# Probabilities times values in float32, two heads of a pair side by side in the array

## The chip, the cores and the metric

One Trainium2 chip, one of its cores. The metric is device time in microseconds; lower is better. The kernel before took 3191.86 us, the median of three runs (3186.04 to 3200.37).

## What is computed

One inference step of a decoder with a convolution layer and an attention layer, for a prompt of 2048 tokens and eight sequences of four new tokens. The change concerns the prompt's attention alone: three groups of eight heads of 64, each group with its own window and dilation. Queries of 128 (a tile) see their own block of 128 keys and the one before:

```python
s = jnp.einsum('...nqd,...nkd->...nqk', qb, k_band, preferred_element_type=jnp.float32) * ATTN_SCALE
s = jnp.where(valid, s, NEG_INF)
mx = jnp.max(s, axis=-1, keepdims=True)
e = jnp.exp(s - mx)
den = jnp.sum(e, axis=-1, keepdims=True)
o = jnp.einsum('...nqk,...nkd->...nqd', e, v_band.astype(jnp.float32)) / den
lse = (mx + jnp.log(den))[..., 0]
```

All is float32. The group outputs are merged later by their `lse`. The last rows of keys and values are outputs too (the caches).

## The kernel before

The program runs in four stages: the convolution's input projections and the convolution (`phase_a`), its output projection (`phase_b`), projections and attention of the three head groups (`phase_c`), merge and output projection (`phase_d`). The framework plans the order of the instructions on each engine with a cost model of its own, before the run, and adds the waits; an engine keeps that order on the chip.

Large products are made in three float32r matmuls: each operand is split into a high half (rounded to float32r) and a low half (the rest), and high x high, high x low and low x high are summed in PSUM. ScalarE (ACT) makes the high half by a copy that rounds, VectorE (DVE) the low half by a subtraction.

`phase_c` calls `attend_group` for each of the three head groups. For each of 16 tiles, `front(i)` loads or transposes the rows of x, projects keys, values and queries (`Trunk.project`, L537 to L540, 24 matmuls each with 512 columns moving), normalises and rotates keys and queries, transposes them and splits them. The values go from PSUM straight into two buffers of three slots: high half by ACT (L769), low half by DVE (L770). For tiles whose rows are part of the cache output, 21 of 48, DVE adds the two halves again (L788) and SyncE (SP) writes the sum out (L789). Then `attention` of the tile before is issued, so that the planner can lay it beside the projections of the next one. Steps of the sample's attention (class `Sample`) are put between; its value products (L708) are plain float32 matmuls of 32 columns, one for each of four tokens, into four partition groups of one bank.

`attention(i, ...)` works on four pairs of heads; e is the head of a pair, and its 64 dimensions are rows 64e to 64e+63 of the transposed queries and keys. `halves` are the key blocks: one (nh = 1) for the first tile of a subsequence, two (nh = 2) for the others. Of the 48 tiles 21 have one block (1, 4 and 16 in the three groups) and 27 have two. Scores (L812) are matmuls of 64 rows, e = 0 and e = 1 in the two halves of the array. DVE adds the mask and finds the maximum (L818), ACT takes the exponential and its sum (L823). Then, part by part (one pair with two blocks, or two pairs with one), PE transposes the probabilities into the bank `pt` (L831), ACT copies them rounded (L834), DVE subtracts for the low half (L835), and three float32r matmuls for each pair and block (L840 to L842) multiply the values of both heads, 128 columns stationary, with the probabilities of both heads, 256 columns moving. Half of that result is needed: rows 0 to 63 for the first head, 64 to 127 for the second. ACT copies the one (L844) and DVE the other (L845) to `uts`. At the tile's end four transposes (L848) turn `uts` into `pu`, DVE copies it to `u` (L849), and `u` is written out.

PSUM banks in the stage: `pj` 3, `tr` 1, and in the first two head groups `s` 2, `pt` 1, `ut` 1 (`ut` and `pu` share the one); in the third `s` 1, `sm` 1 and two that `pt`, `ut` and `pu` share (L891 to L893).

Of the kernel before, what the change touches and what calls it, by code (L numbers as in the profile page):

```python
# [9 lines left out]
F32 = mybir.dt.float32  # L10
F32R = mybir.dt.float32r
AF = mybir.ActivationFunctionType
ALU = mybir.AluOpType
# [211 lines left out]
class Weights:  # L225
# [4 lines left out]
    def __init__(self, tc, d, pool, stage):  # L230
        self.d = d
        self.tc, self.nc, self.pool, self.stage, self.n, self.lo = tc, tc.nc, pool, stage, 0, 0
# [200 lines left out]
class Trunk:  # L433


    def __init__(self, tc, d, kc, pk, pf, pm, psum):
        self.tc, self.nc, self.d, self.pk, self.pool, self.front = tc, tc.nc, d, pk, pf, psum
        self.q, self.p = (pm.tile([128, 2, 2, 512], F32R, tag=t, name="qp_" + t) for t in ("mh0", "ml0"))
        self.turn = [0, 0]
        self.ident, self.mask, self.gk, self.gq = kc.ident, kc.mask, kc.knorm, kc.qnorm  # L440
        self.nkv, self.nb, self.rope_s, self.eps = kc.kvnorm, kc.bnorm, kc.rope_s, kc.eps
        self.ss = kc.ss
        self.rstd = pk.tile([128, 49], F32, name="rstd")
        self.scores = pk.tile([128, 3, 8, TS], F32, name="scores")
        self.sout = pk.tile([TS, 512], F32, name="sout")
# [285 lines left out]
def attend_group(tr, pool, gi, w, kt, vt, state):  # L731

    nc, d = tr.nc, tr.d
# [4 lines left out]
    kvo = d["kvp"][gi].rearrange("(q d) a c -> d q a c", d=dil)  # L738
# [1 line left out]
    nc.sync.dma_start(tab, d["rope"][gi])  # L740
    wk, wv, wq = w
    kth, ktl = kt
    vth, vtl = vt

    def reorder(i, x, nm):

# [9 lines left out]
    def front(i):  # L756
        r, b = divmod(i, nb)
        nm = f"{gi}_{i}"
        s = state["slot"] = (state["slot"] + 1) % 3
        x = tr.rows(gi, i, nm) if gi else tr.flip(i, 128, nm)  # L760
        xt = tr.halves(x)
        col = i + (17 + 16 * (gi - 1) if gi else 0)
        rstd = tr.rstd[:, col:col + 1]
        pk = tr.project(xt, wk, 128, "k" + nm)
        marks = [[tr.first]]
        kn = tr.headnorm(pk, rstd, tr.gk, tab[:, i], 128, "k", nm)
        marks[0] += tr.marks
        pv = tr.project(xt, wv, 128, "v" + nm)
        act = nc.scalar.activation(vth[:, s], pv, AF.Copy, scale=rstd)  # L769
        dve = nc.vector.scalar_tensor_tensor(vtl[:, s], pv, rstd, vth[:, s].bitcast(F32), op0=ALU.mult, op1=ALU.subtract)  # L770
        pq = tr.project(xt, wq, 128, "q" + nm)
        marks.append([tr.first, act, dve])
        qn = tr.headnorm(pq, rstd, tr.gq, tab[:, i], 128, "q", nm)
        if gi < 2:
            reorder(i, x, nm)
        tr.turn[0] ^= 1
        qh, ql = (tr.q[:, tr.turn[0], e].rearrange("p (a b) -> p a b", a=4) for e in range(2))
        for src, h, l, t in ((kn, kth[:, s], ktl[:, s], "k"), (qn, qh, ql, "q")):
            pt = tr.bank("tr", [128, 4, 128], f"p{t}t{nm}")
            for j in range(4):  # L780
                nc.tensor.transpose(pt[:, j], src[:, j * 128:j * 128 + 128], tr.ident)
            nc.scalar.copy(h, pt)
            nc.vector.tensor_tensor(l, pt, h.bitcast(F32), op=ALU.subtract)
        if r + dil * b * 128 >= first:
            o = slice(b * 128 - first // dil, b * 128 - first // dil + 128)
            nc.sync.dma_start(kvo[r, o, 0], kn)
            vo = tr.pool.tile([128, 512], F32, tag="sq", name=f"vo{nm}", bufs=1)
            nc.vector.tensor_tensor(vo, vth[:, s].bitcast(F32), vtl[:, s].bitcast(F32), op=ALU.add)  # L788
            nc.sync.dma_start(kvo[r, o, 1], vo)  # L789
        return (i, s, qh, ql), marks  # L790

    def attention(i, s, qh, ql):
        r, b = divmod(i, nb)
        nm = f"{gi}_{i}"
        p = (s + 2) % 3
        lo_s, hi_s = min(s, p), max(s, p)
        halves = [s] if b == 0 else [lo_s, hi_s]
        nh = len(halves)
# [3 lines left out]
        uts = pool.tile([128, 4, 128], F32, tag="uts", name=f"uts{nm}", bufs=1)  # L802

        rows = [slice(64 * e, 64 * e + 64) for e in range(2)]
        keys = [t[:, s:s + 1] if nh == 1 else t[:, lo_s:hi_s + 1:hi_s - lo_s] for t in (kth, ktl)]
        for js in [range(4)] if nh == 1 else [range(2), range(2, 4)]:

            sc = [tr.bank("s", [128, len(js), nh, 128], f"s{nm}_{js.start}{e}") for e in range(2)]
# [16 lines left out]
            for part in [js[:2], js[2:]] if nh == 1 else [js[:1], js[1:]]:  # L825
                w = len(part)
                pt = tr.bank("pt", [128, nh, w, 2, 128], f"pt{nm}_{part.start}")
                for k, j in enumerate(part):
                    for e in range(2):
                        for m in range(nh):  # L830
                            nc.tensor.transpose(pt[:, m, k, e], sms[e][:, j - js.start, m], tr.ident)  # L831
                tr.turn[1] ^= 1
                ph, pl = (tr.p[:, tr.turn[1], e].rearrange("p (m k e q) -> p m k e q", m=nh, k=w, e=2) for e in range(2))
                nc.scalar.copy(ph, pt)  # L834
                nc.vector.tensor_tensor(pl, pt, ph.bitcast(F32), op=ALU.subtract)  # L835
                ut = tr.bank("ut", [128, w, 2, 128], f"ut{nm}_{part.start}")
                for k, j in enumerate(part):
                    cs = slice(j * 128, j * 128 + 128)
                    for m, sl in enumerate(halves):
                        nc.tensor.matmul(ut[:, k], lhsT=vth[:, sl, cs], rhs=ph[:, m, k], start=(m == 0), stop=False)  # L840
                        nc.tensor.matmul(ut[:, k], lhsT=vth[:, sl, cs], rhs=pl[:, m, k], start=False, stop=False)
                        nc.tensor.matmul(ut[:, k], lhsT=vtl[:, sl, cs], rhs=ph[:, m, k], start=False, stop=(m == nh - 1))  # L842
                out = slice(part.start, part.stop)
                nc.scalar.copy(uts[rows[0], out], ut[rows[0], :, 0])  # L844
                nc.vector.tensor_copy(uts[rows[1], out], ut[rows[1], :, 1])  # L845
        pu = tr.bank("ut", [128, 4, 128], f"pu{nm}")
        for j in range(4):
            nc.tensor.transpose(pu[:, j], uts[:, j], tr.ident)  # L848
# [14 lines left out]
    for i in range(16):  # L863
        nxt, marks = front(i)
# [12 lines left out]
def phase_c(tc, d, tr, wts):  # L877
    nc = tc.nc
    with tc.tile_pool(name="c_p", bufs=2, reuse_waits="tile") as pool, \
            tc.tile_pool(name="c_t", bufs=1, reuse_waits="tile") as pt, ExitStack() as back:  # L880
        kt = [pt.tile([128, 3, 4, 128], F32R, name=f"kt{i}") for i in range(2)]
        vt = [pt.tile([128, 3, 512], F32R, name=f"vt{i}") for i in range(2)]

        def switch(**banks):

# [8 lines left out]
        for gi in range(3):  # L894
            w = [wts.block(d["wkv"][gi], f"k{gi}", tr.nkv), wts.block(d["wkv"][3 + gi], f"v{gi}", tr.nkv),
                 wts.block(d["wq"][gi], f"q{gi}", tr.nb)]
# [226 lines left out]
```

## Time and profile before

| | us |
|---|---|
| median of three runs | 3191.86 |
| the profiled execution's own time | 3187.62 |
| its span in the profile | 3185.8 |
| PE busy | 3054.5 (96%) |
| DVE busy | 2399.4 (75%) |
| ACT busy | 1533.8 (48%) |
| POOL busy | 1282.2 (40%) |

PE is TensorE, PEld its weight loads, POOL is GpSimd, SP the engine that issues most transfers. A busy time is the union of the records of an engine; PE's records overlap, since matmuls are pipelined and their ends are modelled, so what a matmul costs is seen in the distance between starts. A wait is idle time of an engine with what ended it.

### The profile page before, as it was taken

The page shows a single profiled execution, that of the slowest core. Times are in us where ns is not written, and L with a number is a line of the kernel's source. Part 1 is how long each engine was busy: PE and PEld are TensorE (multiplying, and loading weights), DVE is VectorE, ACT ScalarE, POOL GpSimd, SP SyncE. Part 2 cuts the span into 40 slices and gives each one's busy share as a digit, 9 for nine tenths or more (in the row PEclk, how much of TensorE's full clock was granted, in tenths as well). Part 3 has the DMA queues.
Part 4 walks back from the last instruction along what each step waited for, and adds up shares of the span by engine and source line. Part 5 has one row for each costly group of instructions (what it writes and reads, how often), then busy time and mean ns, then how long its engine had stood idle before and what let it go on. Part 6 is the DMA issues. An engine that isn't in the chain of part 4 may idle for free.

```text
span 3185.8 us, 43063 instructions
## 1 busy us (share of the span) xinstructions
PE 3054.5 (96%) x15694; PEld 2633.4 (83%) x15694; DVE 2399.4 (75%) x4067; ACT 1533.8 (48%) x3017; POOL 1282.2 (40%) x809
## 2 busy tenths in 40 slices
PE   6999999999999988999889999999999989999998
PEld 6999999999999976778668888778778777667786
DVE  6699999999989775766467777886678777556455
ACT  6545555554544273656434444644445534444432
POOL 1999988997888230000022222232222031001343
PEclk9999999999999998999989999999999999999999
DMA  6222333333232367566566666886566465552764
GB/s 178 85 85 92 99 120 116 108 104 98 92 145 64 115 216 164 159 174 178 124 183 169 173 175 168 233 218 170 139 147 172 133 186 175 182 174 97 246 235 168
DMA packets 563693, 482.39 MB, mean 151 GB/s; under 512 B 338609, under 2 KB 474417, under 8 KB 555929
## 3 DMA queue, kind: packets, MB, share of 16 engines
q1 hardware_dynamic: 560889, 475.64, 51.7%
q10 hardware_dynamic: 2592, 4.01, 0.3%
q8 instruction: 123, 2.02, 0.3%
q14 instruction: 89, 0.73, 0.1%
HBM read 345.42 MB, written 221.84 MB: 178 GB/s over the span
## 4 chain that ended last, share of the span: by engine, by line
PE 67%; DVE 13%; DMA 11%; ACT 4%; POOL 3%; issue 2%; SPq 1%; ACTq 0%; POOLq 0%; DVEq 0%
PE pg L68 4%; PE pg L70 4%; PE pg L69 4%; PE pv L68 3%; PE pv L70 3%; PE pv L69 3%; PE s L812 3%; PE pz L70 2%; PE pz L68 2%; PE pz L69 2%; DMA bc<-t_c 2%; PE pjq L539 2%; PE pjq L540 2%; PE pjq L537 2%; PE pjk L537 2%; PE pjv L539 2%
## 5 line engine op out<-in xcount | busy, mean ns | idle before, releaser
L181 POOL TENSOR_TENSOR ca<-ca,tp 128x1024 f32<-128x1024 f32 x288 | 705.8, 2453 | 159.2 <-ACT tp L180 108.3
L196 DVE SCALAR_TENSOR_TENSOR acc<-vb,cws,acc 128x1024 f32<-128x1024 f32 x608 | 754.2, 1281 | 6.4
L752 POOL COPY ro<-xt 128x512 f32<-128x512 f32 x128 | 147.6, 1160 | 838.2 <-ACT xt L501 456.9
L180 ACT ACTIVATE tp<-vb,cws 128x1024 f32<-128x1024 f32 x288 | 330.3, 1151 | 295.5 <-POOL ca L181 282.9
L630 POOL TENSOR_TENSOR qb<-qb,kc 128x512 f32<-128x512 f32 x96 | 129.8, 1355 | 335.5 <-DMA qb<-t_qs 252.2
L823 ACT ACTIVATE sm<-sm,ngm 128x256 f32<-128x256 f32 (+1 forms) x384 | 173.2, 453 | 153.8 <-DVE ngm L820 153.2
L68 PE MATMUL pg<-xh,wh 128*128 128x416 f32 x640 | 226.0, 353 | 3.4 <-ACT xh L151 3.4
L70 PE MATMUL pg<-xh,wl 128*128 128x416 f32 x640 | 226.7, 354 | 0.0
L68 PE MATMUL pv<-xh,wh 128*128 128x416 f32 x640 | 225.2, 352 | 1.1 <-DVE vb L109 0.8
L70 PE MATMUL pv<-xh,wl 128*128 128x416 f32 x640 | 226.0, 353 | 0.0
L70 PE MATMUL pz<-xh,wl 128*128 128x416 f32 x640 | 225.9, 353 | 0.0
L69 PE MATMUL pg<-xl,wh 128*128 128x416 f32 x640 | 224.9, 351 | 0.1
L68 PE MATMUL pz<-xh,wh 128*128 128x416 f32 x640 | 224.6, 351 | 0.0
L69 PE MATMUL pv<-xl,wh 128*128 128x416 f32 x640 | 223.6, 349 | 0.0
L69 PE MATMUL pz<-xl,wh 128*128 128x416 f32 x640 | 223.5, 349 | 0.0
L360 PE MATMUL bpo<-ho,bmh 128*128 128x512 f32 x512 | 206.0, 404 | 5.8 <-ACT ho L262 5.8
L361 PE MATMUL bpo<-lo,bmh 128*128 128x512 f32 x512 | 205.9, 403 | 2.6 <-POOL lo L265 2.1
L362 PE MATMUL bpo<-ho,bml 128*128 128x512 f32 x512 | 204.6, 401 | 0.7 <-DVE bml L337 0.7
L812 PE MATMUL s<-kt,qp_mh 64*128 64x256 f32 (+1 forms) x1152 | 164.0, 297 | 4.6 <-DVE u L818 4.1
L812 PEld LDWEIGHTS s<-kt,qp_mh 64*128 64x128 f32 x1152 | 129.7, 189 | 46.9 <-issue 26.1
L537 PE MATMUL pjk<-hk,xt 128*128 128x512 f32 x384 | 160.9, 419 | 0.4 <-DVE ptvs L533 0.4
L539 PE MATMUL pjv<-lv,xt 128*128 128x512 f32 x384 | 156.4, 407 | 0.0
(327 smaller groups left out, 7958.7 us busy)
## 6 DMA issues: line engine op xcount, KB each, us to landing
t_xt<-ro SPq DMA_DIRECT2D x128, 256.0 KB
xt<-t_xt SPq DMA_DIRECT2D x32, 1024.0 KB
wr<-in_win SPq DMA_DIRECT2D x48, 512.0 KB
qb<-t_qs SPq DMA_DIRECT2D x96, 256.0 KB
kc<-in_cache SPq DMA_DIRECT2D x72, 256.0 KB
vc<-in_cache SPq DMA_DIRECT2D x72, 256.0 KB
t_c<-ca SPq DMA_DIRECT2D x16, 1040.0 KB
bc<-t_c SPq DMA_DIRECT2D x16, 1024.0 KB
```

The costliest lines, as they stand in the source:

```text
L68: nc.tensor.matmul(ps, lhsT=hi[:, k], rhs=xh[:, k], start=(k == 0), stop=False)
L69: nc.tensor.matmul(ps, lhsT=hi[:, k], rhs=xl[:, k], start=False, stop=False)
L70: nc.tensor.matmul(ps, lhsT=lo[:, k], rhs=xh[:, k], start=False, stop=(k == 7))
L180: nc.scalar.activation(tp, src, AF.Copy, scale=cws[:, ct, j:j + 1])
L181: nc.gpsimd.tensor_tensor(dst, dst, tp, op=ALU.add)
L196: nc.vector.scalar_tensor_tensor(out if j == KT - 1 else acc[h], vt[:, h * 1024 + j:h * 1024 + j + 1024], cws[:, ct, j:j + 1], out if j == ...
L360: nc.tensor.matmul(po[:n], lhsT=mh[:, a], rhs=hi, start=(a == 0), stop=False)
L361: nc.tensor.matmul(po[:n], lhsT=mh[:, a], rhs=lo, start=False, stop=False)
L362: nc.tensor.matmul(po[:n], lhsT=ml[:, a], rhs=hi, start=False, stop=(a == 15))
L537: first = nc.tensor.matmul(ps[:n], lhsT=xh[:, j], rhs=hi[:, j], start=(k == 0), stop=False)
L539: nc.tensor.matmul(ps[:n], lhsT=xh[:, j], rhs=lo[:, j], start=False, stop=False)
L812: nc.tensor.matmul(sc[e][:, k], lhsT=q[rows[e], j], rhs=keys[t][rows[e], :, j], start=(n == 0), stop=(n == 2))
```

## The change

The values are kept once, in float32, and the probabilities too: the low halves are gone. The result bank `ut` is taken once for a tile, and for each pair and key block there are two float32 matmuls, one per head, with 64 stationary columns and 128 moving ones; they write rows 0 to 63 and 64 to 127 of the same columns of the bank. One ACT copy empties the bank at the tile's end. The cache's value rows are written from the value buffer itself. The buffer of the probabilities has four slots in place of two.

```diff
-        self.q, self.p = (pm.tile([128, 2, 2, 512], F32R, tag=t, name="qp_" + t) for t in ("mh0", "ml0"))
+        self.q = pm.tile([128, 2, 2, 512], F32R, tag="mh0", name="qp_q")
+        self.p = pm.tile([128, 4, 512], F32, tag="ml0", name="qp_p")
...
-        act = nc.scalar.activation(vth[:, s], pv, AF.Copy, scale=rstd)
-        dve = nc.vector.scalar_tensor_tensor(vtl[:, s], pv, rstd, vth[:, s].bitcast(F32), op0=ALU.mult, op1=ALU.subtract)
+        act = nc.scalar.activation(vt[:, s], pv, AF.Copy, scale=rstd)
         pq = tr.project(xt, wq, 128, "q" + nm)
-        marks.append([tr.first, act, dve])
+        marks.append([tr.first, act])
...
             nc.sync.dma_start(kvo[r, o, 0], kn)
-            vo = tr.pool.tile([128, 512], F32, tag="sq", name=f"vo{nm}", bufs=1)
-            nc.vector.tensor_tensor(vo, vth[:, s].bitcast(F32), vtl[:, s].bitcast(F32), op=ALU.add)
-            nc.sync.dma_start(kvo[r, o, 1], vo)
+            nc.sync.dma_start(kvo[r, o, 1], vt[:, s])
...
+        ut = tr.bank("ut", [128, 4, 128], f"ut{nm}")
         for js in [range(4)] if nh == 1 else [range(2), range(2, 4)]:
...
-                tr.turn[1] ^= 1
-                ph, pl = (tr.p[:, tr.turn[1], e].rearrange("p (m k e q) -> p m k e q", m=nh, k=w, e=2) for e in range(2))
-                nc.scalar.copy(ph, pt)
-                nc.vector.tensor_tensor(pl, pt, ph.bitcast(F32), op=ALU.subtract)
-                ut = tr.bank("ut", [128, w, 2, 128], f"ut{nm}_{part.start}")
+                tr.turn[1] = (tr.turn[1] + 1) % 4
+                x = tr.p[:, tr.turn[1]].rearrange("p (m k e q) -> p m k e q", m=nh, k=w, e=2)
+                nc.scalar.copy(x, pt)
+
                 for k, j in enumerate(part):
-                    cs = slice(j * 128, j * 128 + 128)
                     for m, sl in enumerate(halves):
-                        nc.tensor.matmul(ut[:, k], lhsT=vth[:, sl, cs], rhs=ph[:, m, k], start=(m == 0), stop=False)
-                        nc.tensor.matmul(ut[:, k], lhsT=vth[:, sl, cs], rhs=pl[:, m, k], start=False, stop=False)
-                        nc.tensor.matmul(ut[:, k], lhsT=vtl[:, sl, cs], rhs=ph[:, m, k], start=False, stop=(m == nh - 1))
-                out = slice(part.start, part.stop)
-                nc.scalar.copy(uts[rows[0], out], ut[rows[0], :, 0])
-                nc.vector.tensor_copy(uts[rows[1], out], ut[rows[1], :, 1])
+                        for e in range(2):
+                            c = j * 128 + 64 * e
+                            nc.tensor.matmul(ut[rows[e], j], lhsT=vt[:, sl, c:c + 64], rhs=x[:, m, k, e], start=(m == 0), stop=(m == nh - 1))
+        nc.scalar.copy(uts, ut)
         pu = tr.bank("ut", [128, 4, 128], f"pu{nm}")
...
-        vt = [pt.tile([128, 3, 512], F32R, name=f"vt{i}") for i in range(2)]
+        vt = pt.tile([128, 3, 512], F32, name="vt")
```

## Rows read from the trace of the kernel before

**Rows 1.** The page's part 4: the chain that ended last, shares of the span by engine

```profile
PE 67%; DVE 13%; DMA 11%; ACT 4%; POOL 3%; issue 2%; SPq 1%; ACTq 0%; POOLq 0%; DVEq 0%
```

**Rows 2.** Busy time of a stretch: start:end, length, PE, PEld, DVE, ACT, POOL, clock, DMA, GB/s

```profile
1600.00:2994.00 1394.00, 1349.46 (x7211) 1063.22 (x7211) 978.30 (x2766) 629.59 (x1763) 307.83 (x258) 0.98 0.62 171
```

**Rows 3.** Timeline of PE in one stretch: start, duration, engine, line, operation, tiles, count

```profile
1867.99 0.28 PE L840 MATMUL ut<-qp_ml,vt 128*128 128x256 f32 x1
1868.11 0.28 PE L841 MATMUL ut<-qp_ml,vt 128*128 128x256 f32 x1
...
1868.70 0.60 PE L831 MATMUL pt<-ident,sm 128*128 128x128 f32 x4
```

**Rows 4.** Timeline of PE's weight loads in the same stretch

```profile
1868.11 0.19 PEld L842 LDWEIGHTS ut<-qp_ml,vt 128*128 128x128 f32 x1
```

**Rows 5.** Groups by line and shape on PE: count, busy us, mean ns, idle before

```profile
L840 PE MATMUL ut<-qp_ml,vt 128*128 128x256 f32 x300 | 91.4, 305 | 9.5 <-DVE uts L845 6.1 <-ACT qp_ml L834 1.4 <-ACT yq L454 1.0
...
L708 PE MATMUL spo<-vc,spq 128*32 128x512 f32 x192 | 36.8, 602 | 0.0
```

**Rows 6.** Timeline of PE: one whole value product of the sample

```profile
2724.54 1.92 PE L708 MATMUL spo<-vc,spq 128*32 128x512 f32 x16
```

**Rows 7.** Timeline of PE: changes between full-array instructions and others, two places

```profile
1996.77 0.28 PE L842 MATMUL ut<-qp_ml,vt 128*128 128x256 f32 x1
1996.98 0.38 PE L812 MATMUL s<-kt,qp_mh 64*128 64x256 f32 x1
1997.29 0.66 PE L831 MATMUL pt<-ident,sm 128*128 128x128 f32 x4
...
2695.83 0.28 PE L840 MATMUL ut<-qp_ml,vt 128*128 128x256 f32 x1
2696.04 1.06 PE L708 MATMUL spo<-vc,spq 128*32 128x512 f32 x6
2697.03 0.39 PE L841 MATMUL ut<-qp_ml,vt 128*128 128x256 f32 x1
...
2700.17 1.90 PE L708 MATMUL spo<-vc,spq 128*32 128x512 f32 x10
```

**Rows 8.** Timeline of PE: first and last matmul of the 150 value groups

```profile
1643.36 0.38 PE L840 MATMUL ut<-qp_ml,vt 128*128 128x256 f32 x1
...
2991.77 0.28 PE L842 MATMUL ut<-qp_ml,vt 128*128 128x256 f32 x1
```

**Rows 9.** Groups by line and shape on DVE and ACT, 1600 to 3000 us

```profile
L835 DVE TENSOR_TENSOR qp_ml<-pt,qp_ml 128x512 fp32r<-128x512 f32 x150 | 103.2, 688 | 25.8 <-ACT qp_ml L834 24.0
L770 DVE SCALAR_TENSOR_TENSOR vt<-pjv,rstd,vt 128x512 fp32r<-128x512 f32 x47 | 35.1, 746 | 27.5 <-ACT vt L769 27.2
L845 DVE COPY uts<-ut 64x128 f32<-64x128 f32 x108 | 31.8, 295 | 23.7 <-ACT uts L844 20.8
L845 DVE COPY uts<-ut 64x256 f32<-64x256 f32 x42 | 18.0, 428 | 34.4 <-ACT uts L844 33.6
L788 DVE TENSOR_TENSOR vo<-vt,vt 128x512 f32<-128x512 f32 x21 | 15.0, 715 | 0.2
...
L834 ACT CAST qp_ml<-pt 128x512 fp32r<-128x512 f32 x150 | 87.4, 583 | 73.6 <-PE pt L831 72.2
```

**Rows 10.** What PE waited for, 1600 to 3000 us: total, times, longest

```profile
PE pqt L781 <- DVE hnq L565: 6.2, 6, 2.8
PE ut L840 <- DVE uts L845: 6.1, 6, 2.1
PE s L812 <- DVE u L818: 4.1, 4, 1.6
PE ut L841 <- DVE qp_ml L835: 3.8, 5, 1.5
PE pkt L781 <- DVE hnk L565: 3.8, 4, 1.7
PE pu L848 <- DVE uts L845: 2.3, 2, 1.6
```

More of the change, by code (lines that the diff above doesn't have):

```diff
@@ L742, in attend_group @@
     kth, ktl = kt
-    vth, vtl = vt
     def reorder(i, x, nm):
```

## The prediction, made before the changed kernel was run

> **What bounds the kernel now.** I read the views in this order: the chain that ended last, the busy time of the stretch that the change touches, the timeline of TensorE (PE) inside that stretch, then what PE waited for. The chain lies on PE for 67% of the span, with VectorE (DVE) far behind at 13% [rows 1]. All that the change touches runs between 1600 and 2994 us, where three groups of 16 tiles are projected and attended. There PE is busy for 1349.5 of 1394 us and DVE for 978.3, so PE sets the pace and DVE has slack on average [rows 2]. So an instruction taken from PE counts in full there, one taken from DVE only where PE waited for it. PE's busy time is modelled, though: what a matmul really holds is the distance between starts. Six float32r matmuls of one value group start at 1867.99 and the next transposes at 1868.70, so one holds PE for 0.118 us, although its record lasts 0.28 [rows 3]. The loads of their stationary operands hide: the load at 1868.11 starts with the matmul and runs 0.19 us beside it [rows 4].
>
> **Part 1, the product itself.** A tile has four head pairs and one or two key blocks; each "part" of the loop at L825 makes one group of six matmuls (L840 to L842, 128x256 moving). L840 counts 300, two to a group, so there are 150 groups [rows 5]. Today a group costs 6 x 0.118 = 0.71 us. Afterwards it has four calls: two column halves e, for two blocks m (or two pairs k), each with 128 columns moving in plain float32. The nearest rows for such a call are the sample's value products at L708: plain float32, 32 columns stationary, 512 moving, four calls to four column groups. The source makes 96 such calls and the trace has 192 records [rows 5]: each call is two passes. Sixteen of them stand as one piece of 1.92 us, one lasts 0.602, and they start in four waves, so a wave takes (1.92 - 0.602) / 3 = 0.44 us [rows 5, 6]. One behind another they would take 16 x 0.44 = 7.0 us. So passes to different column groups run side by side, and a wave with 512 columns takes 0.44 us, one with 128 a quarter, 0.11 us. The new group has eight passes on two column groups, hence four waves, 0.44 us. That saves 150 x (0.71 - 0.44) = 40 us. A wave could cost as much as today's 0.118: 5 us less saving.
>
> **Part 2, what reshaping the array costs.** The trace shows a price each time PE goes from instructions that fill the array to ones that use part of it, and back. A single score matmul (64 rows) between L842 at 1996.77 and transposes at 1997.29 takes 0.52 us where two normal steps would be 0.24, so 0.28 more, and the transposes behind it are drawn out too. The two waves of L708 between L840 at 2695.83 and L841 at 2697.03 take 1.20 us where 0.12 + 0.88 is work, so 0.20 more, and L841 itself lasts 0.39 instead of 0.28, because its load is laid bare: 0.31 in all [rows 7]. A round trip is thus 0.28 to 0.34 us, a side 0.14 to 0.17. Now the value groups fill the array and pay nothing beside projections and transposes; afterwards every group is a partial one. I went through the 150 groups from 1643.36 to 2991.77 [rows 8] in PE's order: 120 begin behind an instruction that fills the array and 115 end before one; the others touch score matmuls or sample work, where there is a change of shape already. So 235 sides are added. Behind most groups come float32 transposes, whose load is the cheaper one, and a load of 64 columns is half of 128, so I take 0.15: 235 x 0.15 = 35 us lost, with ends of 31 (0.13) and 40 (0.17). Parts 1 and 2 nearly cancel: 40 - 35 = 5 us gained on PE.
>
> **Part 3, what leaves DVE and ScalarE (ACT).** DVE loses the low half of the probabilities (L835, 103.2 us), the low half of the values (L770, 35.1), its half of the output copies (L845, 31.8 + 18.0) and the sum that rebuilt the values for the cache (L788, 15.0): 203 of 978 us [rows 2, 9]. ACT keeps L834 as a copy, loses 150 half copies at L844 and gets 48 copies of 128x512, some 0.58 us each like L834: 28 us [rows 9] on an engine that is busy for 629.6 of 1394 [rows 2]. I cost it at nothing; its cover is the projection matmuls that PE has beside it. If that cover is gone, PE's transposes `pu` wait for a whole copy in place of a half one, about 0.2 us in 48 tiles, 10 us at most.
> What the relief is worth is read from PE's waits. Two belong to what is taken away: `ut` for the copy out of the only bank, 6.1 us, and L841 for the low half, 3.8. Those 9.9 go: afterwards the bank is emptied once per tile, today two to four times. Four more are for DVE's other work: 6.2, 4.1, 3.8 and 2.3, together 16.4 [rows 10]. With a fifth less on DVE I give back a third of them, 5 us. Together 15 us; the ends are nothing (the planner may order the work so that other waits take their place) and 10 + 16 + about 5 for waits hidden under the modelled ends, 31.
>
> **Part 4, edits at nothing.** The value rows for the cache go out of the value tile itself, where today SyncE's issue queues behind DVE's sum; 21 tiles issue it, neither more nor larger transfers than now. It reads a buffer that is written again three tiles later, and a tile takes nearly 30 us (1394 over 48), so nobody waits for it. The square at L549 shares its buffer with that sum and is no longer held by its transfer; that only helps ACT. One `ut` bank is held from a tile's first value group to its copy. In the first two groups of heads it has a bank of its own, as now; in the third it shares two banks with `pt`, and the copy of `pt` to SBUF frees the other in time, with the projection of the next tile as cover. If that cover is gone, the score softmax of the next tile is late; it is in the 10 us above.
>
> **The sum.** -40 + 35 - 15 = -20 us. The profiled execution took 3187.6 us (span 3185.8); the median of the three runs is 3191.9, 4.2 above it. So 3187.6 - 20 + 4.2 = 3172 us, 0.6% below the median. Everything against it at once (waves of 0.118, sides of 0.17, no waits returned, 10 us for the copy): -35 + 40 + 10 = +15, 3207. Everything for it: -40 + 31 - 31 = -40, 3152. A difference under 0.5%, 16 us, can't be told from none here.
>
> **Rivals.**
> *The reshaping eats the gain and no wait comes back.* Only parts 1 and 2 count: -5 us, 3187. For it: PE idles little as it is, and a planned order has other work ready wherever a wait ended; against it: the 9.9 us of waits whose cause is removed.
> *The two halves don't run side by side: slower.* The place is the innermost loop over e. If the second pass of half 0 has to be through before half 1 begins, or the planner puts other work between the two, a group is eight steps of 0.11, 0.88 us against 0.71: +26 us; with the 35 of reshaping and 10 of waits returned +51, so 3243. It decides as soon as the group takes more than 0.71 - 35/150 + 15/150 = 0.58 us. Against it: the four waves of L708 [rows 6]; for it: those are four groups with long moving operands, and L708's own block was broken into six and ten, so that other work came between [rows 7].
> *The loads are laid bare in each wave.* If a pass had to wait for its own load, each of the 600 waves would grow by half of the 0.11 us that a bare load of 128 columns shows [rows 7], 0.055: 33 us, so -20 + 33 = +13, 3205, no visible difference. Against it: today's loads run beside a matmul on the same rows [rows 4]. The Trainium skill, page "TensorE: Matmul & The Clock Gate", section "Part 3: Packing small matmuls — row/col tiling", says that a load overlaps matmuls in flight only when it goes to another row group; by that rule this rival would hold, since both halves use all rows. The trace doesn't bear the rule out for full-array matmuls.
> *More of the waits come back.* PE has 44.5 us idle in the stretch [rows 2]; if most of it goes, -5 - 40 = -45, 3147. Against it: part of it is for transfers that the change leaves alone.
>
> **How the numbers follow.** Forecast (15 us of waits back, 10 to 31) 0.42; reshaping eats it 0.30; bare loads 0.05; halves one after the other 0.15; more waits back 0.08. Faster by over 0.5%: 0.42 + 0.08 = 0.50. Within: 0.30 + 0.05 = 0.35. Slower: 0.15. The range runs from the last rival (3147) to everything against it (3207), with 1 or 2 us of spread between runs on either side: 3146 to 3209. It leaves out the slower rival, 0.15.
>
> **What would show it.** Right: 1200 records of the new matmul in pairs with starts a few ns apart and 0.11 us between pairs, groups of about 0.44 us; steps of some 0.15 us before and after each group; L841's wait for the low half gone; DVE's busy time down by about 200 us and PE's idle time down by some 15. Wrong: single starts 0.11 us apart (halves in turn), pairs at 0.16 (bare loads), value groups broken in two (more than 300 sides), or sides well over 0.17; then the time is the same or slower although DVE is relieved as said.

## The result, and the profile after

The kernel after takes **3149.32 us**, the median of four runs (3143.11 to 3150.16); the kernel before took 3195.93 in runs of the same session. The ratio is 0.985, with an interval of 0.982 to 0.988. Measured again in a later session it was 3140.65, ratio 0.984 (0.982 to 0.986). So it is faster by some 1.5%, 47 us, where 20 had been forecast. The time lies near the low end of the range and beside the price of the last rival (3147), but not for that rival's reason, as the waits will show.

The chain that ended last, by engine, has moved further onto PE [rows 1]:

```profile
PE 71%; DMA 12%; DVE 10%; ACT 3%; POOL 2%; issue 2%; SPq 1%; POOLq 0%; ACTq 0%; DVEq 0%
```

The busy time of the attention stage (start:end, length, PE, PEld, DVE, ACT, POOL, granted clock, DMA share, GB/s) answers to [rows 2]:

```profile
1600.00:2960.00 1360.00, 1315.89 (x7532) 989.75 (x7531) 791.14 (x2414) 621.42 (x1669) 310.79 (x260) 0.98 0.64 177
```

The stretch is 34 us shorter, DVE's busy time 187 us less, about the 203 of the prediction. The clock is the same 0.98, so it plays no part. PE's idle time is 1360.00 - 1315.89 = 44.1 us after 44.5, but the two stretches don't hold the same work: in this execution the stage's first score matmul starts at 1623.08, before it was 1613.43, and 4.8 us of the idle time lie ahead of it. From the first score matmul to the last value matmul, before and after:

```profile
1613.43:2991.77 1378.34, 1334.50 (x7153) 1054.42 (x7152) 970.35 (x2744) 624.50 (x1751) 307.83 (x258) 0.98 0.62 172
...
1623.08:2957.04 1333.96, 1295.44 (x7452) 977.33 (x7452) 774.98 (x2377) 611.87 (x1649) 307.01 (x258) 0.98 0.64 176
```

**PE's idle time falls from 43.8 to 38.5 us, so some 5 came back.** The profile of the later session has 37.8 us between the same two matmuls.

PE's groups in the same stage (count | busy us, mean ns of one | idle before it and what ended it) show the new product at L838 and the scores, L810 now and L812 before:

```profile
L838 PE MATMUL ut<-qp_p,vt 128*64 128x128 f32 x1200 | 100.2, 287 | 2.8 <-ACT qp_p L832 2.7
L810 PE MATMUL s<-kt,qp_q 64*128 64x256 f32 x648 | 77.0, 308 | 0.5 <-DVE u L816 0.5
L810 PE MATMUL s<-kt,qp_q 64*128 64x128 f32 x504 | 64.5, 286 | 6.3 <-DVE u L816 6.2
```

The same two groups of scores in the kernel before:

```profile
L812 PE MATMUL s<-kt,qp_mh 64*128 64x256 f32 x648 | 95.2, 307 | 1.3 <-DVE u L818 0.9
L812 PE MATMUL s<-kt,qp_mh 64*128 64x128 f32 x504 | 68.9, 283 | 3.3 <-DVE u L818 3.2
```

There are 1200 records for 600 calls, so a float32 call is two passes, as read off the sample's product [rows 5]. And the score matmuls, which the diff leaves alone, have lost 18 us of busy time in the first group. That was not foreseen.

One value group in the timeline of PE (start, duration, engine, line, operation, tiles, count), to be held against [rows 3]:

```profile
1909.96 0.39 PE L540 MATMUL pjk<-lk,xt 128*128 128x512 f32 x1
1910.28 0.66 PE L838 MATMUL ut<-qp_p,vt 128*64 128x128 f32 x8
1910.87 0.66 PE L829 MATMUL pt<-ident,sm 128*128 128x128 f32 x4
1911.28 0.48 PE L541 MATMUL pjk<-hk,xt 128*128 128x512 f32 x1
```

Eight passes lie in 0.66 us. Inside, they start in four pairs, 6 ns apart; the first pair stands alone for 0.16 us, the others follow 0.109 apart. From the projection to the first pair it is 0.32 us, where one projection follows another after 0.23, and from the last pair to the transposes 0.20, where 0.11 would do. PE's weight loads in the same place:

```profile
1910.28 0.42 PEld L838 LDWEIGHTS ut<-qp_p,vt 128*64 128x64 f32 x8 [0.36 <-ACT qp_q L781]
```

The eight loads begin with the group and take 0.42 us together, beside the passes. So a group costs about what part 1 said, and both its sides have a price, as part 2 said.

Since PE's busy time is modelled, I add up the distances between starts instead, from the first score matmul to the last value matmul. Each distance is given the normal step of the instruction that opens it: 0.233 us for a projection, 0.109 for a transpose, 0.117 for a value matmul before, 0.109 for a wave of two halves, 0.215 for a float32 pass of 256 columns (below), 0.117 or 0.110 for a score step. What a change of the array's shape adds, up to 0.11 us in the distance that holds the change and up to 0.11 in the next, is "reshaping"; what is still over is "rest" (waits, issue and whatever else lengthens a distance). A score step is one start distance, whether one matmul or two side by side begin there. The cap of 0.11 is a choice: with caps from 0.08 to 0.22 the difference in reshaping lies between +24 and +27 us, and the rest moves the other way.

| kernel | stretch, us | value product | scores | reshaping (changes) | rest |
|---|---|---|---|---|---|
| before | 1378.3 | 105.2 | 112.7 | 72.2 (444) | 78.2 |
| after | 1334.0 | 65.9 | 98.2 | 99.1 (621) | 63.3 |
| difference | -44.3 | -39.3 | -14.5 | +26.9 (+177) | -14.9 |

Another 3 us go in the sample's product. (The two profiled executions as wholes differ by 38.5 us only, since the stage starts 9.7 us later in the one after; in the later session's profile it starts at 1612.50.) This account carries the result: the product gave 39, the scores 14, the rest 15, and reshaping took back 27. A change of shape costs 0.163 us before and 0.160 after. Of the rest, the distances between two value matmuls with no change of shape near give the most: 9.9 us over the normal step before, 0.5 after. Only 5 of the 15 us are idle time in the profile, since the modelled ends cover short waits; what the other 10 are was not followed further.

Why the scores? They run in pairs, one in each half of the array's rows, when the two heads of a pair stand close to each other in PE's order; experiment 8 forces that order and gets the pairs. In the timeline of the kernel before a group of twelve takes:

```profile
1725.47 1.67 PE L812 MATMUL s<-kt,qp_mh 64*128 64x256 f32 x12
...
1668.90 0.97 PE L812 MATMUL s<-kt,qp_mh 64*128 64x256 f32 x12
```

and in the kernel after:

```profile
1735.64 1.31 PE L810 MATMUL s<-kt,qp_q 64*128 64x256 f32 x12
...
2028.35 0.97 PE L810 MATMUL s<-kt,qp_q 64*128 64x256 f32 x12
```

0.97 us is six pairs; 1.67 is eleven steps, with one pair among them. The 648 matmuls of 256 columns took 520 steps before and 416 after, 104 fewer at 0.117 = 12 us. The scores also hold together better: they stand in 157 unbroken runs in place of 189, and the value products in 150 in place of 189. A run that isn't broken has two changes of shape fewer. So of the 235 sides that the prediction added, 247 arose (value product beside an instruction that fills the array), but changes between scores and the full array fell from 368 to 261: 621 - 444 = 177 net. The order on each engine is planned ahead of the run, and the relieved plan is another one.

PE's largest waits in the stage (total us, times, longest):

```profile
PE px L500 <- DMA xr<-t_x: 13.6, 15, 4.1
PE s L810 <- DVE u L816: 6.7, 5, 2.5
PE pqt L780 <- DVE hnq L566: 5.5, 5, 1.6
PE pkt L780 <- DVE hnk L566: 5.4, 4, 2.5
...
PE ut L838 <- ACT qp_p L832: 2.7, 2, 1.8
...
PE pu L842 <- ACT uts L839: 0.7, 1, 0.7
```

The two waits whose cause was removed, 6.1 and 3.8 us [rows 10], are gone. But the wait of the scores for DVE's `u` went from 4.1 to 6.7, and that of the value matmuls for ACT's copy of the probabilities from 1.4 [rows 5] to 2.7. (Of the 5.4 of `pkt` 2.5 lie ahead of the first score matmul.) Other waits have filled about half of the place.

### The profile page after: what moved, and what is told of

Same layout as the page of the kernel before. It is cut to its first block, busy times and chain, and to the rows that moved or that the text cites. A ratio compares the mean times of both kernels' runs of the same rounds, so it can differ in the third digit from the quotient of the medians.

```text
span 3147.3 us, 43062 instructions
## 1 busy us (share of the span) xinstructions
PE 3019.0 (96%) x15994; PEld 2558.8 (81%) x15994; DVE 2202.9 (70%) x3698; ACT 1522.5 (48%) x2915; POOL 1283.9 (41%) x809
## 4 chain that ended last, share of the span: by engine, by line
PE 71%; DMA 12%; DVE 10%; ACT 3%; POOL 2%; issue 2%; SPq 1%; POOLq 0%; ACTq 0%; DVEq 0%
PE pz L70 4%; PE pz L68 4%; PE pz L69 4%; PE pv L68 3%; PE pv L70 3%; PE pg L68 3%; PE pv L69 3%; PE pg L70 3%; PE pg L69 3%; PE s L810 3%; PE pjk L538 2%; PE pjk L540 2%; DMA qb<-t_qs 2%; PE pjk L541 2%; PE pt L829 2%; PE pjv L538 2%
## 5 line engine op out<-in xcount | busy, mean ns | idle before, releaser
L832 ACT COPY qp_p<-pt 128x512 f32<-128x512 f32 x150 | 87.5, 584 | 201.8 <-PE pt L829 201.5
L538 PE MATMUL pjk<-hk,xt 128*128 128x512 f32 x384 | 161.4, 420 | 0.0
L540 PE MATMUL pjk<-lk,xt 128*128 128x512 f32 x384 | 158.0, 411 | 0.0
L541 PE MATMUL pjk<-hk,xt 128*128 128x512 f32 x384 | 156.3, 407 | 0.0
```

The source lines that it names most:

```text
L538: first = nc.tensor.matmul(ps[:n], lhsT=xh[:, j], rhs=hi[:, j], start=(k == 0), stop=False)
L540: nc.tensor.matmul(ps[:n], lhsT=xh[:, j], rhs=lo[:, j], start=False, stop=False)
L541: nc.tensor.matmul(ps[:n], lhsT=xl[:, j], rhs=hi[:, j], start=False, stop=(k == last))
```

## Experiments

Theory: (a) the product is cheap because two column halves run side by side, (b) a change of the array's shape costs PE time (0.14 us in the expectations, from 85.0 us over 621 changes; the rule of the table above gives 99.1 us, 0.16 for each), and (c) the low halves on DVE made PE's order worse. Rivals: it is DVE's time, or the one bank and one copy, or float32 in itself. Three sessions ran them, each beside the kernel before: experiments 1 to 4 beside 3193.96 us, 5 to 8 beside 3189.88, 9 to 11 beside 3194.11. Across sessions the ratios to before are compared (after: 0.985 and 0.984).

**1. DVE's subtractions back.** Each of the 150 groups gets a subtraction whose result nobody reads.

```diff
                 nc.scalar.copy(x, pt)
+                lo = tr.lo[:, tr.turn[1] % 2].rearrange("p (m k e q) -> p m k e q", m=nh, k=w, e=2)
+                nc.vector.tensor_tensor(lo, pt, x, op=ALU.subtract)
```

> The kernel after, with the 150 subtractions on VectorE put back; their result is read by nobody, so TensorE does not wait for them. VectorE's busy time should rise by 150 x 0.69 = 103 us. Theory 'VectorE's time': if the score matmuls hold together better because VectorE is less busy, half of the relief is taken back here, score runs go up again from 157 towards 189, and the time rises by 10 to 20 us, to 3160 to 3170 us. Theory 'the wait': if it is the wait of the value matmuls for the low half that broke the order, nothing of it comes back, and the time stays within 5 us of 3149 us.

Measured: 3141.50, ratio 0.985 (0.984 to 0.986), not to be told from after. The groups of the two lines concerned:

```profile
L834 DVE TENSOR_TENSOR lo<-pt,qp_p 128x512 f32<-128x512 f32 x150 | 103.0, 686 | 72.5 <-ACT qp_p L832 71.7
...
L810 PE MATMUL s<-kt,qp_q 64*128 64x256 f32 x648 | 80.3, 309 | 0.6 <-DVE u L816 0.5
```

103 us of DVE are back and cost nothing. DVE's time is not what the change saved; the scores keep their 157 runs.

**2. The kernel before without the low half of the probabilities.** The second of its three matmuls reads the high half again.

```diff
-                nc.vector.tensor_tensor(pl, pt, ph.bitcast(F32), op=ALU.subtract)
...
-                        nc.tensor.matmul(ut[:, k], lhsT=vth[:, sl, cs], rhs=pl[:, m, k], start=False, stop=False)
+                        nc.tensor.matmul(ut[:, k], lhsT=vth[:, sl, cs], rhs=ph[:, m, k], start=False, stop=False)
```

> The kernel before, without the 150 subtractions; the second of the three value matmuls reads the high half once more, so the low half of the probabilities is left out of the product and TensorE's own work is unchanged (900 matmuls of 128x256). Both theories that see the gain in the order of TensorE's work expect it here in part: fewer score runs than 189, a time 15 to 25 us under before, about 3172 to 3180 us. If the whole gain is the product itself (value matmuls 104.8 to 67.9 us on TensorE), this run is within 5 us of before.

Measured: 3172.82, ratio 0.994 (0.992 to 0.995). PE has every matmul that it had before, and yet the kernel is some 20 us faster. The scores' group shows where:

```profile
L812 PE MATMUL s<-kt,qp_mh 64*128 64x256 f32 x648 | 85.2, 307 | 3.8 <-DVE u L818 3.8
```

By start distances: value product 105.2 as before, scores 107.0 (-5.7), reshaping 64.6 with 388 changes (-7.6), rest 74.6 (-3.6). Score runs 159. PE's idle time is 47.0 us, not less than the 43.8 before. So what the relief is worth is mostly order on PE, not waits. In experiment 1 the subtraction is back and the order holds: it isn't the subtraction alone either.

**3. One head after the other.** The loop over e outside the one over m, so that all passes of one half precede the other half in the program.

```diff
-                    for m, sl in enumerate(halves):
-                        for e in range(2):
+                    for e in range(2):
+                        for m, sl in enumerate(halves):
```

> The kernel after, with the two heads of a pair in turn: all calls of head 0 of a pair, then all of head 1. With one key block nothing changes in the order of a pair (84 pairs of calls); with two blocks (108 groups) four passes of one half come before four of the other. If TensorE takes passes only in the order given, such a group is four steps of 0.11 us, then four more beside nothing, with one pass overlapping in the middle: 0.77 us in place of 0.44, so 108 x 0.33 = 36 us more, about 3185 us. If it can look four passes ahead to the other column half, the groups stay at 0.44 us and the time at 3149 us.

Measured: 3145.29, ratio 0.986 (0.984 to 0.987). A value group in the timeline:

```profile
1904.11 0.66 PE L838 MATMUL ut<-qp_p,vt 128*64 128x128 f32 x8
1904.71 0.66 PE L829 MATMUL pt<-ident,sm 128*128 128x128 f32 x4
```

Still 0.66 us. In the program's order on PE the four passes of head 0 come first in such a group, and the first pass of head 1 starts 13 ns after the first of head 0. So it is in 104 of the 149 value runs, 13 or 14 ns; in most others, groups with one key block whose order the edit leaves alone, it is 6 or 7 ns, as in the kernel after. The halves run side by side without being alternated.

**4. Float32 without the halves.** One call for both heads, as before: 128 columns stationary, 256 moving, a bank and two copies per part.

```diff
-                        for e in range(2):
-                            c = j * 128 + 64 * e
-                            nc.tensor.matmul(ut[rows[e], j], lhsT=vt[:, sl, c:c + 64], rhs=x[:, m, k, e], start=(m == 0), stop=(m == nh - 1))
+                        nc.tensor.matmul(ut[:, k], lhsT=vt[:, sl, cs], rhs=x[:, m, k], start=(m == 0), stop=(m == nh - 1))
```

> The values and probabilities in plain float32 as in the kernel after, but the product in the form of before: both heads at once, 128 columns stationary, 256 moving, one bank and two copies per part. No reshaping of the array. A call is two passes of 256 columns, 0.22 us each, so a group is 4 x 0.22 = 0.88 us against 0.71 before and 0.44 after. With VectorE relieved of 153 us and no wait for a low half. Theory 'the order': the better order of the scores (25 us) is kept, +26 us for the product: about 3195 us, no change against before. Theory 'all of the gain is the product in column halves': 3195 + 26 = 3220 us.

Measured: 3170.23, ratio 0.993 (0.992 to 0.994), less than either theory had. The group and one of its places in the timeline:

```profile
L836 PE MATMUL ut<-qp_p,vt 128*128 128x256 f32 x600 | 159.4, 388 | 6.5 <-ACT qp_p L831 3.6 <-DVE uts L839 2.7 <-DVE u L843 0.2
```

```profile
1906.48 1.02 PE L836 MATMUL ut<-qp_p,vt 128*128 128x256 f32 x4
1907.34 0.60 PE L828 MATMUL pt<-ident,sm 128*128 128x128 f32 x4
```

Four passes hold PE from 1906.48 to 1907.34, 0.215 us each: 600 x 0.215 = 129 us, 24 more than before. Against that, reshaping falls to 64.5 (386 changes, -8), the scores to 95.2 (-17), the rest to 64.1 (-14). The expectation had the dearer product and missed part of the better order and the whole of the rest. Within the change, then, the column halves are worth 129 - 65.9 = 63 us of product and cost 35 of reshaping; the float32 form without them is already ahead of before, through the order and the rest.

**5. Two parts in one run.** The value products of two parts are issued together, so PE enters the column form half as often.

```diff
-                for k, j in enumerate(part):
...
+                later.append((part, x))
+            first = None
+            for part, x in reversed(later):
+                with ExitStack() as behind:
+                    if first is not None:
+                        behind.enter_context(tr.tc.issue_after(first.ins))
+                    for k, j in enumerate(part):
...
+                                first = nc.tensor.matmul(ut[rows[e], j], lhsT=vt[:, sl, c:c + 64], rhs=x[:, m, k, e], start=(m == 0), stop=(m == nh - 1))
```

> The kernel after, with the value matmuls of two parts issued as one run (the later part's first, since its operand is ready last, the earlier part's right behind). Same work, same waits for the copies, but about 77 value runs in place of 150, and about 140 fewer changes of the array's shape in TensorE's order. Theory 'a change of shape costs 0.14 us on TensorE and TensorE sets the pace' (85 us for 621 changes in the trace after): 20 us less, about 3128 us. Theory 'the change is hidden among waits that would be there anyway': within 5 us of 3146 us, or slower, because the value matmuls come later.

Measured: 3112.13, ratio 0.976 (0.974 to 0.978), 0.8 to 1.0% below after, 26 to 31 us; the stretch of the account is 1308.8, 25 shorter. 77 value runs in place of 150; 485 changes in place of 621, and reshaping 76.8 in place of 99.1: 22.3/136 = 0.164 us for each change that is gone. The busy time of the value product falls with it, from 100.2:

```profile
L844 PE MATMUL ut<-qp_p,vt 128*64 128x128 f32 x1200 | 83.2, 280 | 3.0 <-ACT qp_p L832 3.0
```

**6. A bank and two copies per part.** After, with that one thing as before.

```diff
+                ut = tr.bank("ut", [128, w, 128], f"ut{nm}_{part.start}")
...
+                nc.scalar.copy(uts[rows[0], out], ut[rows[0]])
+                nc.vector.tensor_copy(uts[rows[1], out], ut[rows[1]])
-        nc.scalar.copy(uts, ut)
```

> The kernel after, but with a result bank for each part and its two half copies (ACT and VectorE), as before. VectorE gets 108 x 0.30 + 42 x 0.43 = 50 us of copies back, TensorE has to wait again for the bank to be emptied up to four times a tile. Prediction's step 'the 6.1 us of waits for the only bank come back': 6 to 12 us slower than the 3146 us of the kernel after. Theory 'TensorE has other work beside every such wait': within 5 us.

Measured: 3147.76, ratio 0.987 (0.985 to 0.989), 0.1 to 0.3% above after, within the intervals; the stretch of the account is 1336.8, between 1334.0 and 1337.0 in two executions of after. PE's waits in the stage:

```profile
PE ut L837 <- ACT qp_p L831: 3.6, 2, 3.0
...
PE pu L843 <- DVE uts L840: 3.1, 3, 1.6
```

No `ut` waits for a copy out, although the bank is again emptied per part. The one bank and one copy are worth nothing that can be measured here, and the 6.1 us of bank waits before didn't come from having a bank per part alone.

**7. The wait for DVE put back.** Experiment 4 with the 150 subtractions; the second call of each group reads their result, so part of the product is left out.

```diff
+                lo = tr.lo[:, tr.turn[1] % 2].rearrange("p (m k e q) -> p m k e q", m=nh, k=w, e=2)
+                nc.vector.tensor_tensor(lo, pt, x, op=ALU.subtract)
...
-                        nc.tensor.matmul(ut[:, k], lhsT=vt[:, sl, cs], rhs=x[:, m, k], start=(m == 0), stop=(m == nh - 1))
+                        nc.tensor.matmul(ut[:, k], lhsT=vt[:, sl, cs], rhs=(x, lo)[m + k][:, m, k], start=(m == 0), stop=(m == nh - 1))
```

> The kernel with the full-array float32 product (3170 us), with VectorE's 150 subtractions put back and the second call of each group reading their result, as the second and third matmul did before: the group is ready in two steps again. (The low half stands in for the probabilities in that call, so part of the product is left out.) VectorE's 103 us alone cost nothing in an earlier run. Theory 'the wait': value runs go up from 151 to about 185 and scores are torn apart again, 15 to 25 us slower, 3185 to 3195 us. Theory 'the wait costs little by itself': 3170 to 3176 us.

Measured: 3173.87, ratio 0.995 (0.993 to 0.997), against 0.993 in experiment 4: some 5 us more, with overlapping intervals; the stretch is 1367.8 against 1360.9. The second call and its wait:

```profile
L838 PE MATMUL ut<-lo,vt 128*128 128x256 f32 x300 | 92.0, 389 | 3.6 <-DVE lo L833 3.5
```

The value runs are broken again (185), the scores only little (165). So DVE's subtraction and the wait behind it together cost 5 to 7 us by these medians, which the overlapping intervals don't set apart from nothing; neither DVE's time (1) nor this wait (7) carries the 20 us of experiment 2 alone.

**8. Scores forced into pairs.** Experiment 5, with the score matmuls of the first two head groups chained so that the heads alternate, at a raised priority.

```diff
-                    for e in range(2):
-                        nc.tensor.matmul(sc[e][:, k], lhsT=q[rows[e], j], rhs=keys[t][rows[e], :, j], start=(n == 0), stop=(n == 2))
+                    for e in ((1, 0) if gi < 2 else (0, 1)):
+                        with ExitStack() as behind:
+                            if prev is not None and gi < 2:
+                                behind.enter_context(tr.tc.issue_after(prev.ins))
+                            behind.enter_context(tr.tc.high_priority(offset=100))
+                            prev = nc.tensor.matmul(sc[e][:, k], lhsT=q[rows[e], j], rhs=keys[t][rows[e], :, j], start=(n == 0), stop=(n == 2))
```

> The kernel with value runs of two parts, and the score matmuls with two banks chained so that the two heads of a pair alternate, with a somewhat higher priority. Planned: some 355 steps for the 648 score matmuls of 256 columns in place of 441, and as many changes of shape as without it, within 20. If two score matmuls of a pair that stand side by side share one step of 0.117 us, and TensorE sets the pace: 86 x 0.117 = 10 us less than the run with two parts alone. If VectorE, which empties the score banks, is late for the forced order: no gain or a loss.

Measured: 3134.31, ratio 0.984 (0.982 to 0.986), 22 us slower than experiment 5. The scores did fall, from 96.7 to 90.4 us (407 steps of 256 columns to 355), but the rest rose from 61.4 to 92.4. Most of that is PE's idle time, from 38.6 to 57.0, in these waits among others:

```profile
PE px L500 <- DMA xr<-t_x: 28.8, 16, 4.7
PE pt L834 <- ACT qp_p L837: 6.8, 12, 0.9
```

Pairing is real and worth 6 us here; forcing it took more than it gave, since work that would have covered a transfer was now behind the scores.

**9. The kernel before without the low half of the values.** L770 and the sum L788 go, and the third matmul reads the high half.

```diff
-        dve = nc.vector.scalar_tensor_tensor(vtl[:, s], pv, rstd, vth[:, s].bitcast(F32), op0=ALU.mult, op1=ALU.subtract)
...
-                        nc.tensor.matmul(ut[:, k], lhsT=vtl[:, sl, cs], rhs=ph[:, m, k], start=False, stop=(m == nh - 1))
+                        nc.tensor.matmul(ut[:, k], lhsT=vth[:, sl, cs], rhs=ph[:, m, k], start=False, stop=(m == nh - 1))
```

> The kernel before without the low half of the values on VectorE (L770, 35 us) and without the sum that rebuilt them (L788, 15 us); the third value matmul reads the high half again, so the low half of the values is left out of the product and of the cache rows. TensorE's own work is unchanged. Leaving out the 150 subtractions for the low half of the probabilities took 21 us. Theory 'any wait taken off the value groups lets TensorE's order hold together': here nothing that a value group waits for goes, the planned score runs stay at 187, so within 8 us of before. Theory 'VectorE's time': 50 us of VectorE's work should bring half of what 103 us brought, about 10 us.

Measured: 3184.14, ratio 0.997 (0.996 to 0.999), about 9 us. The runs stay broken (187 and 188) and the scores stay dear:

```profile
L809 PE MATMUL s<-kt,qp_mh 64*128 64x256 f32 x648 | 93.7, 306 | 7.4 <-DVE u L815 6.7
```

So the values' low half doesn't carry the better order. The time itself decides little: 9 us lies between the "within 8" of the one theory and the "about 10" of the other.

**10. The whole tile in one run.** After, with all value products of a tile at its end, as in experiment 5 but with the list opened ahead of the loop over js and emptied behind it.

```diff
         ut = tr.bank("ut", [128, 4, 128], f"ut{nm}")
+        later = []
...
+                later.append((part, x))
+        first = None
+        for part, x in reversed(later):
```

> The kernel after, with all value matmuls of a tile in one run at its end: 48 to 50 value runs in place of 75 in the run with two parts and 150 in the kernel after; planned changes of shape 429 against 472 and 612. If each change costs 0.14 us on TensorE: 43 x 0.14 = 6 us under the run with two parts, about 3106 us. If the value matmuls, coming later, delay the end of the tile and the slots of the probabilities hold back the next tile: above 3112 us.

Measured: 3105.74 (3102.30 to 3109.11), ratio 0.973 (0.971 to 0.975), as expected and the fastest version here, 35 us below after in the same session. 50 value runs, 442 changes, reshaping 70.9. Its interval overlaps that of experiment 5, so the step from two parts to four is in the expected direction but not clear of noise. All of a tile's 32 passes stand together:

```profile
1927.21 1.97 PE L845 MATMUL ut<-qp_p,vt 128*64 128x128 f32 x32
```

The first of the 16 pairs takes 0.16 us, the next fourteen 0.109 each, and the last record is 0.28 long.

**11. Both heads in one column half.** Experiment 3 with both results written to rows 0 to 63: the same passes, loads and changes of shape, but no two halves to run side by side. The second head's result replaces the first's, so half of the output is not computed.

```diff
-                            nc.tensor.matmul(ut[rows[e], j], lhsT=vt[:, sl, c:c + 64], rhs=x[:, m, k, e], start=(m == 0), stop=(m == nh - 1))
-        nc.scalar.copy(uts, ut)
+                            nc.tensor.matmul(ut[rows[0], j], lhsT=vt[:, sl, c:c + 64], rhs=x[:, m, k, e], start=(m == 0), stop=(m == nh - 1))
+        nc.scalar.copy(uts[rows[0]], ut[rows[0]])
+        nc.vector.tensor_copy(uts[rows[1]], ut[rows[0]])
```

> The kernel after, with the matmuls of both heads sent to the same column half of the array (rows 0 to 63 of the bank; the second head's result takes the place of the first's, so half of the output is not computed, and the copy reads the same rows twice). The passes can't run side by side: a group is eight steps of 0.11 us, 0.87, in place of 0.44. If running side by side is what makes the new product cheap, 150 x 0.43 = 65 us more than the kernel after, about 3210 us, slower than before. If something else in the change carries the gain, less than 20 us more.

Measured: 3196.65, ratio 1.001 (1.000 to 1.003): 56 us above the kernel after in the same session (3140.65), and the whole gain of the change is gone. One group, and the line:

```profile
1943.77 1.09 PE L838 MATMUL ut<-qp_p,vt 128*64 128x128 f32 x8
```

```profile
L838 PE MATMUL ut<-qp_p,vt 128*64 128x128 f32 x1200 | 161.8, 279 | 1.4 <-ACT qp_p L832 1.4
```

Eight steps of 0.109 us in place of four; over the stage the product takes 130.7 us in place of 65.9. Without the two halves the change would have been worth nothing. This is the condition of the "slower" rival; the kernel came out level with before and not at 3243, because the product cost 26 us more, as priced, but reshaping only 21 more (93.0), and the scores 18 less (94.2).

## Why the prediction was right, and where it was not

- *Part 1, the product: right.* -40 said, -39.3 measured; the waves are 0.109 us as derived from the sample's 512-column product, and the first of each group is longer. Experiment 11 shows that the halves side by side are the reason.
- *Part 2, reshaping: price right, number too high.* 0.15 per side was taken; 99.1/621 = 0.160 (before: 72.2/444 = 0.163) and 0.164 from experiment 5 bear it out. One reason given for 0.15 does not hold: a load of 64 columns takes 0.137 us in the trace after, the transposes' load of 128 takes 0.140, not twice as much. And 247 sides between value product and full array did arise. But the step "so 235 sides are added" counted these in the order of the kernel before and kept every other change of shape where it was. The new order has 107 fewer changes between scores and the full array, others rose by 37, so 177 came net, and the cost was 27 us where 35 had been said.
- *Part 3, waits: size met, reason only in part.* 15 us were said and the rest fell by 14.9. But PE's idle time fell by 5 alone: the two named waits went, 9.9 us, and others took about half of their place. The remaining 10 us came out of distances that the profile doesn't show as idle; the prediction had 5 of that kind, and only at its favourable end. Experiments 1 and 6 show that neither DVE's time nor the bank is worth anything by itself. That the sum of 15 was met is luck in part.
- *Not in the prediction: the scores.* -14 us from pairs that stand side by side more often. For the stage: -39 + 27 - 14 - 15 - 3 = -44 (product, reshaping, scores, rest, the sample's product), where the forecast had -40 + 35 - 15 = -20. The scores and the smaller reshaping make most of the difference, which carried the time to the low end of the range.
- *Part 4: right.* The ACT copies (L839) and the cache's rows cost nothing that shows: `pu` waits 0.7 us in all for them.
- *Rivals.* "Reshaping eats the gain": refuted, since product and reshaping alone come to -12 us and the time is 47 us lower. "Halves in turn": refuted by the pairs 6 ns apart. "Bare loads": refuted by waves of 0.109 us; only the first of a group takes 0.16. The Trainium skill, page "TensorE: Matmul & The Clock Gate", section "Part 3: Packing small matmuls — row/col tiling", has loads overlap only towards another row group; here both halves use all 128 rows and the loads hide behind the passes all the same, but for the first of a group. "More waits come back" gave 3147 and the result was 3149, but its mechanism did not happen: 38.5 of 43.8 us of idle time are still there. The number alone would have confirmed a false reason.

What stays open is why the planned order improves. It is not additive over the removed pieces: DVE's subtraction alone 0 us (1), the subtraction with its wait 5 to 7, if anything (7), the values' low half 9 (9), the probabilities' low half 20 (2). Which dependence the planner trips over was not settled. The four slots of the probabilities' buffer were in every version built on the kernel after and were never tried by themselves; experiment 2 has two slots and the better score runs, so they are not needed for those.

## What to carry to other kernels

A product of which only half the result is needed can go to the two column halves of the array, one head each: in float32 that halves its time on PE (65.9 us against 130.7 here), but every change between the full array and a part of it cost about 0.16 us here, so put partial-array work into long runs. On this kernel one run for each tile was worth another 1.1% (3105.7 us against 3140.7). Where an order is planned, an edit is priced with the order it will bring: look at how runs of instructions of one shape are broken, and not only at waits.

## What the hardware showed that was not expected

- PE starts work for another column half ahead of its turn: with the heads one after the other in the program, the second head's first pass starts 13 ns after the first head's, past three passes still due (experiment 3). The Trainium skill, in the same section of "TensorE: Matmul & The Clock Gate", says that matmuls start strictly in the program's order; this trace does not agree.
- A plain float32 call is two passes, and a pass of 256 columns steps at 0.215 us, of 128 at 0.109; a float32r matmul of 256 columns steps at 0.117. So a full-array float32 product (2 x 0.215) costs only 23% more than three float32r ones (3 x 0.117), and needs no low halves.
- Two score matmuls of 64 rows run side by side only when they stand close together in the order: twelve take 0.97 us in six pairs and 1.67 nearly all single.
- A change between the full array and a part of it costs 0.16 us in the table's two kernels. Page "TensorEngine Tiling (Array Packing)", section "Key Properties", of the Trainium skill says that a change of the tiling mode drains the engine; the 0.16 us for each change seen here fit that.
